# Differential attention: one wide product per head instead of two, and norm factors that travel through DRAM

## The chip, the cores and the metric

The kernel runs on one core of a Trainium2 chip. The metric is the device time of one execution in microseconds. The profile of one execution is used beside it; its times count from the first instruction.

The engines are TensorE (PE, with its weight loads PEld), VectorE (DVE), ScalarE (ACT), GpSimd (POOL) and SyncE (SP). SP issues all DMAs of the kernel before. Matrix products go into PSUM banks of 128 partitions by 512 floats; the other engines read them from there.

## The reference

The model is one layer of an encoder, run on two sequences of 512 tokens (`x_prompt`, `x_sample`), width 1024. Three branches work on the normalised input: a state space scan, a differential attention, and a cross attention to 256 memory tokens. Each goes through its up-projection and a gate; their sum goes through an output projection and a feed-forward part. The change lies in the differential attention:

```python
def block(qblk):                       # 128 queries at a time
    s = jnp.einsum('bqhd,bkhd->bhqk', qblk, k).astype(jnp.float32) * scale
    probs = jax.nn.softmax(s, axis=-1).reshape(Bn, DIFF_HEADS, 2, Q_BLOCK, L)
    w = probs[:, :, 0] - lam * probs[:, :, 1]
    return jnp.einsum('bhqk,bkhe->bqhe', w.astype(v.dtype), v)
...
o = _rmsnorm(o, subln_g) * (1.0 - lambda_init)     # over the 128 columns of a head
```

There are 4 heads, each with two score maps of depth 64 and values of depth 128. After the weighted sum over v each token's 128 values of a head are divided by their root mean square: one factor for each token, head and sequence.

## The kernel before, in words

Matrices are split into a high and a low part in the reduced float type (fp32r), and each product is three matmuls (high by high, high by low, low by high). `split` makes the parts: a copy on ScalarE for the high part, a subtraction on DVE for the low one. `weight` (L143 to L150) loads a weight tile through SP into one of two buffers wf and splits it into wh and wl.

The differential attention is one loop over `steps`: 4 heads, 2 sequences and 4 query tiles of 128 make 32 steps. A (head, sequence) pair takes four steps in a row. Within a pair, `qt` runs from 0 to 3. The work of a step is spread over several turns of the loop:

- `scores` runs on every second turn, for two query tiles at a time. PE makes the scores of both maps, DVE the row maxima (nb), ScalarE the exponentials, DVE the weighted difference of the maps (e0).
- `turn` transposes the 128x512 difference on PE, four transposes into one bank of the tag tr, and splits it into pH and pL.
- `outputs` multiplies v by those. It works on two query tiles at once: 12 matmuls of 256 columns, run at every odd `qt`. The two halves share one PSUM bank (oo), and after the second half ScalarE copies it to `osb`, a 128x512 tile with the head's depth on the partitions and the tokens along the columns.
- `squares`, two turns after a pair's last step, transposes `osb`, so that ScalarE can sum the squares of a token's values; the result `ss` is 128x4, with a token on each partition.
- `normed`, three turns after a pair's last step, calls `factor`: square root on ScalarE, reciprocal on DVE (rs, 128x4), and then four transposes on PE, which lay the factor of every token along the columns and repeat it on all 128 partitions, in a second bank of the tag tr (bc). DVE multiplies `osb` by it, and SP stores the result to bD in DRAM.

Between these parts `fill(n)` puts other matmuls into PE's list from a queue: projections of q and k of the next heads, projections of v, gate projections, and towards the end of the loop the merge of the other branches. `fill(n)` takes about n matmuls of 512 columns. While this loop is built, PE keeps its instructions in the order in which they are written (`PE.on`). The order on the other engines and on SP is chosen by a scheduler, which may be held back with `issue_after`; `queued()` places a DMA after the last weight load.

There are two PSUM banks of the tag tr (shared by `scores`, `turn`, `squares` and the broadcast of the factors), two of mm for the filling matmuls, three of sc and one of oo. `osb` has two buffers, and so has the tag acc, which `squares` uses for its squares.

After the loop, `merge_in(1)` loads bD[1] back from DRAM.

Of the kernel before, what the change touches and what calls it, by code (L numbers as in the profile page):

```python
# [10 lines left out]
F32 = mybir.dt.float32  # L11
F32R = mybir.dt.float32r
I32 = mybir.dt.int32
AF = mybir.ActivationFunctionType
ALU = mybir.AluOpType
# [4 lines left out]
P = 128  # L20
L = 512
# [51 lines left out]
def encoder(ctx: ExitStack, tc: tile.TileContext, a, out):  # L73
    nc = tc.nc
    V, S, PO, PE = nc.vector, nc.scalar, nc.gpsimd, InOrder(tc, nc.tensor)
# [8 lines left out]
    rp = ctx.enter_context(tc.tile_pool(name="rp", bufs=2))  # L84
# [3 lines left out]
    def open_tags(es, side=None, **tags):  # L88

        for tag, n in tags.items():  # L90
            pools[tag] = es.enter_context(tc.tile_pool(name=tag, bufs=n, side=side, reuse_waits="tile"))
# [10 lines left out]
    xp_es, phase = ExitStack(), ExitStack()  # L102
    open_tags(xp_es, side="right", xp=2 * KD)
    drp = ctx.enter_context(tc.tile_pool(name="drp", bufs=1, space=DRAM))

    def slot(tag, shape=(P, NT), dt=F32, name="sl"):
        return pools[tag].tile(list(shape), dt, tag=tag, name=name)

    def bank(tag="mm"):
        return pools[tag].tile([P, 512], F32, tag=tag, name="bk" + tag)  # L110

    def aux():
        return bank("tr")
# [17 lines left out]
    def split(hi, lo, src, scale=None):  # L131

        if scale is None:
            h = S.copy(hi, src)  # L134
            l_ = V.tensor_tensor(out=lo, in0=src, in1=hi.bitcast(F32), op=ALU.subtract)  # L135
        else:
            h = S.activation(out=hi, in_=src, func=AF.Copy, scale=scale)
            l_ = V.scalar_tensor_tensor(out=lo, in0=src, scalar=scale, in1=hi.bitcast(F32), op0=ALU.mult, op1=ALU.subtract)
        return h, l_
# [23 lines left out]
    def proj(src, hi, lo, nk=KD, seqs=(0, 1)):  # L163


        wh, wl = weight(src, nk * P)
        outs = []
        for s in seqs:
            cs = slice(s * L, (s + 1) * L)
            outs.append(bank())  # L170
            for k in range(nk):
                mm3(outs[-1:], wh, wl, [(hi[k][:, cs], lo[k][:, cs])], k, nk)
        return outs
# [10 lines left out]
    def new_acc():  # L184
        return rp.tile([P, L], F32, tag="acc", name="acc", bufs=2)

    def rstd(acc, n, nt=4):


        ss = aux()  # L190
        for t in range(nt):
            PE.matmul(ss[:, t : t + 1], acc[:, t * P : (t + 1) * P], onec[:, 0:1], start=(t == 0), stop=(t == nt - 1))
        return factor(ss, n, nt)

    def factor(ss, n, nt=4, bias=epsc):

        rs = rp.tile([P, 4], F32, tag="rs", name="rs", bufs=4)
        S.activation(out=rs[:, :nt], in_=ss[:, :nt], func=AF.Sqrt, scale=1.0 / n, bias=bias)
        V.reciprocal(rs[:, :nt], rs[:, :nt])
        bc = aux()  # L200
        for t in range(nt):
            PE.transpose(bc[:, t * P : (t + 1) * P], rs[:, t : t + 1].broadcast_to([P, P]), ident)
        return rs, bc
# [26 lines left out]
    def sums(src, tag="wb", ss=None, ts=range(4)):  # L230

        nonlocal last_sq
        if ss is None:
            ss = rp.tile([P, 4], F32, tag="ss", name="ss", bufs=3)
        for t in ts:
            tk = slot(tag, [P, DM], name="tk")
            nc.sync.dma_start(tk, src[t])
            last_sq = S.activation(out=tk, in_=tk, func=AF.Square, accum_out=ss[:, t : t + 1])
        return ss
# [53 lines left out]
    def queued():  # L293

        return tc.issue_after(last_w.ins)
# [54 lines left out]
    with yielding(last_s):  # L350
        x_norm(0, norm[0], range(5, 8))
        _, bc = factor(ss1, DM)
# [30 lines left out]
    for t2 in range(2):  # L383
# [3 lines left out]
        for s in range(NS):  # L387
            for t in range(2):
                o = bank()
# [126 lines left out]
    with behind():  # L516
# [3 lines left out]
        rs_, bc = factor(sums(a["memN"], "ld"), DM)  # L520
# [4 lines left out]
    for t in range(4):  # L525
        o = proj(a["w_glu"][t], zh, zl, 4)
# [32 lines left out]
    g04 = cst.tile([P, 1], F32, name="g04")  # L559
# [38 lines left out]
    def fill(n):  # L598
        nonlocal owed
        owed += n  # L600
        while owed > 0 and queue:
            r = next(queue[0], None)
            if r is None:
                queue.pop(0)
            else:
                owed -= r
        if not queue:
            owed = 0

    def finish(g):  # L610
        while any(g is g_ for g_ in queue):
            fill(1)
# [75 lines left out]
    steps = [(h, s, lt) for h in range(4) for s in range(NS) for lt in range(4)]  # L688
    es, pT = {}, {}
    AHEAD = 2  # L690
    for i in range(-AHEAD, len(steps) + 1):
        if i + AHEAD < len(steps):
            h, s, lt = steps[i + AHEAD]
# [9 lines left out]
            last_e = last_x, V.tensor_scalar_mul(e, e, r)  # L703
            es[i + AHEAD] = e
        fill(9 if i == 0 else 5)
        if 0 <= i < len(steps):
            h, s, lt = steps[i]
# [3 lines left out]
            tr = aux()  # L711
# [4 lines left out]
        if i > 0 and steps[i - 1][2] == 3:  # L716
            h, s, _ = steps[i - 1]
            pTh, pTl = pT.pop((h, s))
            oo = bank("oo")
# [5 lines left out]
            osb = xa.tile([P, L], F32, tag="osb", name="xosb", bufs=1)  # L725
# [7 lines left out]
    phase.close()  # L733


    open_tags(phase, v2=2, qk=12, pT=4)
    aes = ExitStack()
    ap_ = aes.enter_context(tc.tile_pool(name="att", bufs=2, reuse_waits="tile"))
    acol = aes.enter_context(tc.tile_pool(name="acol", bufs=2, reuse_waits="tile"))
# [21 lines left out]
    qk = {}  # L761
# [40 lines left out]
    def first_in():  # L802
        b0.append(merge_in(0, ["qk", "qk", "qk", "v"]))
        yield 0
# [25 lines left out]
    s0, ss, osb = {}, {}, {}  # L830
# [22 lines left out]

    def turn(i):
        h, s, qt = steps[i]
        if qt % 2 == 0:
            pT[h, s, qt // 2] = tuple(slot("pT", [P, 4, 2 * P], F32R, n_) for n_ in ("pH", "pL"))
        e0 = es.pop(i)
        tr = aux()
        for j in range(4):  # L860
            PE.transpose(tr[:, j * P : (j + 1) * P], e0[:, j * P : (j + 1) * P], ident)
        ps = slice(qt % 2 * P, qt % 2 * P + P)
        split(*(p_[:, :, ps] for p_ in pT[h, s, qt // 2]), tr.rearrange("p (j q) -> p j q", j=4))

    def outputs(i):

        h, s, qt = steps[i]
        if h == 2 and s == qt - 1 == 0:
            finish(v1_)
        vh, vl = (v1 if h >= 2 else v0)[s]  # L870
        vs = slice((h % 2) * P, (h % 2) * P + P)
        pH, pL = pT.pop((h, s, qt // 2))
        if qt == 1:
            osb[h, s] = bank("oo")
        od = osb[h, s][:, qt // 2 * 2 * P : (qt // 2 + 1) * 2 * P]
        for j in range(4):
            PE.matmul(od, vh[:, j, vs], pH[:, j, :], start=(j == 0), stop=False)
            PE.matmul(od, vh[:, j, vs], pL[:, j, :], start=False, stop=False)
            PE.matmul(od, vl[:, j, vs], pH[:, j, :], start=False, stop=(j == 3))
        if qt == 3:  # L880
            o_ = rp.tile([P, L], F32, tag="nsq", name="osb", bufs=2)
            S.copy(o_, osb[h, s])
            osb[h, s] = o_

    def squares(i):
        h, s, _ = steps[i]
        tr = aux()
        ss[h, s] = rp.tile([P, 4], F32, tag="ss", name="ss", bufs=3)
        for t in range(4):
            PE.transpose(tr[:, t * P : (t + 1) * P], osb[h, s][:, t * P : (t + 1) * P], ident)  # L890
        sq = new_acc()
        for t in range(4):
            S.activation(out=sq[:, t * P : (t + 1) * P], in_=tr[:, t * P : (t + 1) * P], func=AF.Square,
                         accum_out=ss[h, s][:, t : t + 1])
        V.scalar_tensor_tensor(out=s0[h, s], in0=s0[h, s], scalar=EPS * P, in1=s0[h, s], op0=ALU.mult, op1=ALU.mult)
        V.tensor_tensor(out=ss[h, s], in0=ss[h, s], in1=s0[h, s], op=ALU.add)

    def normed(i):
        h, s, _ = steps[i]
        _, bc = factor(ss[h, s], P, bias=0.0)  # L900
        V.scalar_tensor_tensor(out=osb[h, s], in0=osb[h, s], scalar=g04, in1=bc, op0=ALU.mult, op1=ALU.mult)
        nc.sync.dma_start(bD[1, h, :, s * L : (s + 1) * L], osb[h, s])

    n = len(steps)
    for i in range(-1, n + 3):
        if i % 2 and i + 1 < n:
            scores(i + 1)
        if i == 22:
            queue.insert(1, first_in())
        fill(10 if i < n - 1 else 16)  # L910
        if 0 <= i < n:
            turn(i)
        if 0 < i <= n and steps[i - 1][2] % 2:
            outputs(i - 1)
        fill(10)
        if 1 < i <= n + 1 and steps[i - 2][2] == 3:
            squares(i - 2)
        if i > 2 and steps[i - 3][2] == 3:
            normed(i - 3)
    aes.close()  # L920
    while queue:
        fill(24)
# [212 lines left out]
    for i in range(KFF):  # L1135
# [14 lines left out]
        ps = products(i, w)  # L1150
        p0 = next(ps)
        if i == 0:
            for s in range(NS):
                _, bc = rstd(accs[s], DM)
# [92 lines left out]
    for v, (m, lo_, hi_) in enumerate(VISITS):  # L1247
        ps = [bank() for _ in range(6)] + [aux()]
# [22 lines left out]
        ps = iter(ps)  # L1271
# [62 lines left out]
    for c, n in ((0, L), (L, L // 2), (L + L // 2, L // 2)):  # L1334
        acc = new_acc()
        for m in range(KD):
# [6 lines left out]
            o = bank()[:, :n]  # L1343
# [12 lines left out]
            if m == KD - 3:  # L1356
                ss = aux()
# [435 lines left out]
```

## Time and profile before

| | us |
|---|---|
| median of 3 runs | 1598.61 |
| lowest, highest | 1598.05, 1599.04 |
| the profiled execution's own time | 1599.28 |
| its span, from first to last instruction | 1597.5 |
| the loop of the differential attention, roughly | from 494 to 770 |

Granted clock of TensorE in the profiled execution: 0.998 of full speed.

How to read the rows in the next part: rows of groups give an engine, an operation, the tile written and the tile read, the shapes, the count, the busy time and the mean duration of one in nanoseconds. Rows in order of time give the start, the length, and in brackets the engine's idle time before it with what ended it. A matmul's own length overlaps with the next one's, so what PE pays for one is the distance from its start to the next start. Rows of DMAs give the issuing queue, the size of one, and the median time from issue to landing. "x12" behind a row counts the instructions merged in it.

### The profile page before, as it was taken

Reading aid. Unit: us, or ns where it says so; the run is one execution under the profiler, and the core shown is the slowest. Engines: PE = TensorE matmul, PEld = TensorE weight load, DVE = VectorE, ACT = ScalarE, POOL = GpSimd, SP = SyncE. Lnnn points to the kernel's source line nnn. Section 1 sums busy time; section 2 is a strip of 40 time slices with the busy share of each in tenths; the row PEclk is TensorE's granted clock in tenths of the full one; section 3 lists DMA queues with packets and bytes.
Section 4 is the critical chain, followed back from the end, with each engine's and each line's share of the span. In section 5 each row is a group of like instructions: output and inputs, shape, how many; then the busy total and the mean of one; then the engine's idle time right before and its main releaser. Section 6 shows DMA issues by size and latency. Waiting matters only on the chain.

```text
span 1597.5 us, 21606 instructions
## 1 busy us (share of the span) xinstructions
PE 1579.1 (99%) x7838; PEld 1314.8 (82%) x7838; DVE 1163.7 (73%) x1856; ACT 636.8 (40%) x1140; POOL 542.6 (34%) x449
## 2 busy tenths in 40 slices
PE   9999999999999999999999999999999999999997
PEld 7888788888898789878878878888888888788877
DVE  7976997067774776775365578888898778998654
ACT  6544313265552465573123443323333224233323
POOL 0010100001333220300443366666665553444553
PEclk9999999999999999999999999999999999999999
DMA  9544523676762111253454432333332223985222
GB/s 366 174 159 152 175 94 123 182 261 213 262 224 102 46 55 40 73 178 133 138 190 140 144 108 89 123 122 129 119 116 109 81 91 115 355 332 196 75 67 106
DMA packets 104890, 237.84 MB, mean 149 GB/s; under 512 B 13520, under 2 KB 45008, under 8 KB 104784
## 3 DMA queue, kind: packets, MB, share of 16 engines
q1 hardware_dynamic: 104784, 236.47, 43.4%
q8 instruction: 61, 1.00, 0.2%
q14 instruction: 45, 0.37, 0.1%
HBM read 165.16 MB, written 71.27 MB: 148 GB/s over the span
## 4 chain that ended last, share of the span: by engine, by line
PE 89%; DVE 5%; issue 2%; DMA 2%; POOL 1%; ACT 1%; SPq 0%; POOLq 0%; DVEq 0%; ACTq 0%
PE bkmm L66 78%; PE bktr L66 3%; DVE tl L135 2%; PE bkoo L66 2%; PE bktr L69 2%; PE bksc L66 1%; PE bktr L1627 1%; PE bktr L1598 1%; PE bktr L1688 0%; PE bktr L1686 0%; PE bktr L1687 0%; PE bktr L1566 0%; DMA acc<-in_w_fo 0%; DMA mt<-in_memT 0%; DMA fl<-aD 0%
## 5 line engine op out<-in xcount | busy, mean ns | idle before, releaser
L66 PE MATMUL bkmm<-xh,wh 128*128 128x512 f32 x640 | 254.7, 398 | 0.0
L66 PE MATMUL bkmm<-xh,wl 128*128 128x512 f32 x640 | 251.1, 393 | 0.0
L66 PE MATMUL bkmm<-xl,wh 128*128 128x512 f32 x640 | 250.5, 391 | 0.0
L66 PE MATMUL bkmm<-tl,wh 128*128 128x512 f32 (+1 forms) x621 | 241.3, 389 | 1.4 <-DVE tl L135 1.4
L66 PE MATMUL bkmm<-th,wl 128*128 128x512 f32 (+1 forms) x621 | 241.1, 389 | 1.0 <-DVE wl L135 1.0
L66 PE MATMUL bkmm<-th,wh 128*128 128x512 f32 (+1 forms) x621 | 241.3, 389 | 0.0
L134 ACT CAST wh<-wf 128x1024 fp32r<-128x1024 f32 (+1 forms) x134 | 117.9, 880 | 220.8 <-PE bkmm L66 183.2
L135 DVE TENSOR_TENSOR wl<-wf,wh 128x1024 fp32r<-128x1024 f32 (+1 forms) x134 | 146.5, 1093 | 48.8 <-ACT wh L134 33.5
L66 PE MATMUL bkmm<-th,w 128*128 128x512 f32 x432 | 141.4, 392 | 3.5 <-DVE up L1102 2.0
L66 PEld LDWEIGHTS bkmm<-xh,wl 128*128 128x128 f32 x640 | 120.2, 188 | 26.6 <-issue 1.3
L66 PEld LDWEIGHTS bkmm<-xh,wh 128*128 128x128 f32 x640 | 120.4, 188 | 26.4 <-issue 3.4
L66 PEld LDWEIGHTS bkmm<-xl,wh 128*128 128x128 f32 x640 | 120.5, 188 | 22.6 <-issue 0.4
L66 PEld LDWEIGHTS bkmm<-tl,wh 128*128 128x128 f32 x621 | 116.6, 188 | 26.2 <-DVE tl L135 2.1
L66 PEld LDWEIGHTS bkmm<-th,wl 128*128 128x128 f32 x621 | 116.6, 188 | 25.6 <-DVE wl L135 1.9
L66 PEld LDWEIGHTS bkmm<-th,wh 128*128 128x128 f32 x621 | 116.6, 188 | 23.7
L1166 POOL TENSOR_TENSOR up<-up,acc 128x512 f32<-128x512 f32 x44 | 84.2, 1931 | 87.4 <-DVE up L1102 87.4
L454 POOL TENSOR_TENSOR raw<-raw 128x128 f32<-128x128 f32 x28 | 15.2, 546 | 285.0 <-DVE nb L545 206.5
L66 PEld LDWEIGHTS bkmm<-th,w 128*128 128x128 f32 x432 | 80.9, 188 | 24.9 <-DVE up L1102 4.5
L793 POOL TENSOR_TENSOR mg<-mg,gl 128x1024 f32<-128x1024 f32 x16 | 43.5, 2720 | 138.1 <-DVE gl L789 138.1
L66 PE MATMUL bkmm<-tl,w 128*128 128x512 f32 x216 | 84.2, 390 | 0.0
L66 PE MATMUL bkmm<-yh,wh 128*128 128x512 f32 x192 | 75.9, 397 | 0.8 <-DVE gl L789 0.8
L1165 ACT ACTIVATE ac<-gf 128x512 f32<-128x512 f32 x44 | 27.8, 633 | 122.5 <-DVE gf L1164 63.5
(651 smaller groups left out, 3580.8 us busy)
## 6 DMA issues: line engine op xcount, KB each, us to landing
wf<-in_w_in SPq DMA_DIRECT2D x40, 512.0 KB, 4.1
wD<-hl SPq DMA_DIRECT2D x28, 512.0 KB, 2.9
w<-wD SPq DMA_DIRECT2D x28, 512.0 KB, 4.8
gD<-gt SPq DMA_DIRECT2D x24, 512.0 KB, 2.8
gl<-gD SPq DMA_DIRECT2D x24, 512.0 KB, 3.4
wf<-in_w_fg SPq DMA_DIRECT2D x22, 512.0 KB, 3.7
wf<-in_w_fu SPq DMA_DIRECT2D x22, 512.0 KB, 3.6
aD<-ac SPq DMA_DIRECT2D x22, 512.0 KB, 3.0
```

What stands on the lines that cost most here:

```text
L66: return self.put(self.eng.matmul(*args, **kw))
L69: return self.put(self.eng.transpose(*args, **kw))
L134: h = S.copy(hi, src)
L135: l_ = V.tensor_tensor(out=lo, in0=src, in1=hi.bitcast(F32), op=ALU.subtract)
L454: PO.tensor_tensor(out=a22, in0=a21, in1=a22, op=ALU.add)
L793: PO.tensor_tensor(out=mg[m], in0=mg[m], in1=gt, op=ALU.add)
L1165: last_t = S.activation(out=ac[:, cs], in_=gf, func=AF.Tanh, scale=0.5)
L1166: PO.tensor_tensor(out=up, in0=up, in1=accs[s], op=ALU.mult)
L1598: PE.matmul(kp[64 * hf : 64 * hf + 48, g * 144 : (g + 1) * 144], l_[:, 2 * hf + g, :], o_[:, 4 * g4 + 2 * hf + g, :], start=(l_ is lr48), ...
L1627: PE.matmul(ps[:, g * P : (g + 1) * P], w_[:, gg * P : (gg + 1) * P], u_[:, 8 * o + gg, :], start=True, stop=True)
```

## The change

The products with v of a pair are made in one run of 12 matmuls of 512 columns, after all four query tiles have been transposed. The transposed probabilities of a pair lie in one tile of 512 columns for each part; there are two such tiles (high and low) instead of four of half the width. The products come before the transposes of the next pair's first tile, and the fill around them is shifted by four matmuls (14 and 6 instead of 10 and 10).

The norm factors of all pairs but the last take another way. `factors` makes rs as before, three turns after the pair's last step, without the transposes on PE. One turn later SP writes it to DRAM (`spread_out`), transposed, so that 512 factors lie in a row: 512 single floats from 128 partitions. One turn after that the row is read back on all 128 partitions into a tile of the tag acc (`spread_in`); this DMA is issued by ScalarE, behind the exponentials of the last scores. Two turns after that `normed` multiplies `osb` by it. The last pair keeps `factor` and its transposes.

```diff
-    open_tags(phase, v2=2, qk=12, pT=4)
+    open_tags(phase, v2=2, qk=12, pT=2)
...
     def turn(i):
         h, s, qt = steps[i]
-        if qt % 2 == 0:
-            pT[h, s, qt // 2] = tuple(slot("pT", [P, 4, 2 * P], F32R, n_) for n_ in ("pH", "pL"))
+        if qt == 0:
+            pT[h, s] = tuple(slot("pT", [P, 4, L], F32R, n_) for n_ in ("pH", "pL"))
...
-        ps = slice(qt % 2 * P, qt % 2 * P + P)
-        split(*(p_[:, :, ps] for p_ in pT[h, s, qt // 2]), tr.rearrange("p (j q) -> p j q", j=4))
+        ps = slice(qt * P, qt * P + P)
+        split(*(p_[:, :, ps] for p_ in pT[h, s]), tr.rearrange("p (j q) -> p j q", j=4))
...
     def outputs(i):
...
-        pH, pL = pT.pop((h, s, qt // 2))
-        if qt == 1:
-            osb[h, s] = bank("oo")
-        od = osb[h, s][:, qt // 2 * 2 * P : (qt // 2 + 1) * 2 * P]
+        pH, pL = pT.pop((h, s))
+        od = bank("oo")
         for j in range(4):
             PE.matmul(od, vh[:, j, vs], pH[:, j, :], start=(j == 0), stop=False)
             PE.matmul(od, vh[:, j, vs], pL[:, j, :], start=False, stop=False)
             PE.matmul(od, vl[:, j, vs], pH[:, j, :], start=False, stop=(j == 3))
-        if qt == 3:
-            o_ = rp.tile([P, L], F32, tag="nsq", name="osb", bufs=2)
-            S.copy(o_, osb[h, s])
-            osb[h, s] = o_
+        osb[h, s] = rp.tile([P, L], F32, tag="nsq", name="osb", bufs=2)
+        S.copy(osb[h, s], od)
...
+    rD = drp.tile([2 * 4, 4, P], F32, name="rD")
+    far = {}
+
+    def factors(i):
+        h, s, _ = steps[i]
+        if i == n - 1:
+            far[h, s] = factor(ss[h, s], P, bias=0.0)[1]
+            return
+        rs = far[h, s] = rp.tile([P, 4], F32, tag="rs", name="rs", bufs=4)
+        S.activation(out=rs, in_=ss[h, s], func=AF.Sqrt, scale=1.0 / P, bias=0.0)
+        V.reciprocal(rs, rs)
+
+    def spread_out(i):
+        h, s, _ = steps[i]
+        with queued():
+            nc.sync.dma_start(rD[2 * h + s].rearrange("t p -> p t"), far[h, s])
+
+    def spread_in(i):
+        h, s, _ = steps[i]
+        far[h, s] = new_acc()
+        with tc.issue_after(last_e[0].ins):
+            nc.scalar.dma_start(far[h, s], rD[2 * h + s : 2 * h + s + 1].rearrange("o t p -> o (t p)").broadcast_to([P, L]))
+
     def normed(i):
         h, s, _ = steps[i]
-        _, bc = factor(ss[h, s], P, bias=0.0)
-        V.scalar_tensor_tensor(out=osb[h, s], in0=osb[h, s], scalar=g04, in1=bc, op0=ALU.mult, op1=ALU.mult)
+        V.scalar_tensor_tensor(out=osb[h, s], in0=osb[h, s], scalar=g04, in1=far[h, s], op0=ALU.mult, op1=ALU.mult)
         nc.sync.dma_start(bD[1, h, :, s * L : (s + 1) * L], osb[h, s])
...
-        fill(10 if i < n - 1 else 16)
+        due = 0 < i <= n and steps[i - 1][2] == 3
+        fill((10 if i < n - 1 else 16) + 4 * due)
+        if due:
+            outputs(i - 1)
         if 0 <= i < n:
             turn(i)
-        if 0 < i <= n and steps[i - 1][2] % 2:
-            outputs(i - 1)
-        fill(10)
+        fill(10 - 4 * due)
         if 1 < i <= n + 1 and steps[i - 2][2] == 3:
             squares(i - 2)
+        if i > 6 and steps[i - 7][2] == 3:
+            with tc.issue_after(last_e[1].ins):
+                normed(i - 7)
         if i > 2 and steps[i - 3][2] == 3:
-            normed(i - 3)
+            factors(i - 3)
+            if i == n + 2:
+                normed(i - 3)
+        if i > 3 and i - 4 < n - 1 and steps[i - 4][2] == 3:
+            spread_out(i - 4)
+        if i > 4 and i - 5 < n - 1 and steps[i - 5][2] == 3:
+            spread_in(i - 5)
```

More of the change, by code (lines that the diff above doesn't have):

```diff
@@ L861, in turn @@
             PE.transpose(tr[:, j * P : (j + 1) * P], e0[:, j * P : (j + 1) * P], ident)
-        ps = slice(qt % 2 * P, qt % 2 * P + P)
-        split(*(p_[:, :, ps] for p_ in pT[h, s, qt // 2]), tr.rearrange("p (j q) -> p j q", j=4))
+        ps = slice(qt * P, qt * P + P)
+        split(*(p_[:, :, ps] for p_ in pT[h, s]), tr.rearrange("p (j q) -> p j q", j=4))
     def outputs(i):
-        h, s, qt = steps[i]
-        if h == 2 and s == qt - 1 == 0:
+        h, s, _ = steps[i]
+        if h == 2 and s == 0:
             finish(v1_)
@@ L896, in squares @@
         V.tensor_tensor(out=ss[h, s], in0=ss[h, s], in1=s0[h, s], op=ALU.add)
+    rD = drp.tile([2 * 4, 4, P], F32, name="rD")
[13 more added lines that the diff above has]
+    def spread_in(i):
+        h, s, _ = steps[i]
+        far[h, s] = new_acc()
+        with tc.issue_after(last_e[0].ins):
+            nc.scalar.dma_start(far[h, s], rD[2 * h + s : 2 * h + s + 1].rearrange("o t p -> o (t p)").broadcast_to([P, L]))
     def normed(i):
         h, s, _ = steps[i]
-        _, bc = factor(ss[h, s], P, bias=0.0)
-        V.scalar_tensor_tensor(out=osb[h, s], in0=osb[h, s], scalar=g04, in1=bc, op0=ALU.mult, op1=ALU.mult)
+        V.scalar_tensor_tensor(out=osb[h, s], in0=osb[h, s], scalar=g04, in1=far[h, s], op0=ALU.mult, op1=ALU.mult)
         nc.sync.dma_start(bD[1, h, :, s * L : (s + 1) * L], osb[h, s])
```

## The prediction

> **What bounds the kernel now.** I read the page first, then the stretches of time around the differential attention, then who PE waits for there, then the chain that ended last, then single rows on PE, ScalarE (ACT), VectorE (DVE) and SyncE's queue (SP). The page:
>
> ```profile
> span 1597.5 us, 21606 instructions
> PE 1579.1 (99%) x7838; PEld 1314.8 (82%) x7838; DVE 1163.7 (73%) x1856; ACT 636.8 (40%) x1140; POOL 542.6 (34%) x449
> PEclk9999999999999999999999999999999999999999
> PE 89%; DVE 5%; issue 2%; DMA 2%; POOL 1%; ACT 1%; SPq 0%; POOLq 0%; DVEq 0%; ACTq 0%
> ```
>
> PE is busy for 99% of the span at a full clock, and the chain that ended last is 89% PE. All edits lie in the loop that runs from about 494 to 770 us. Busy time in that stretch, by engine, in the order PE, PEld, DVE, ACT, POOL, then clock, DMA share, GB/s; and below it the only wait of PE's matmuls in this part that the profile names:
>
> ```profile
> 494.00:770.00 276.00, 275.20 (x1552) 228.12 (x1551) 182.97 (x339) 136.54 (x313) 51.04 (x33) 1.00 0.25 85
> ...
> PE bktr L69 <- DVE osb L901: 0.8, 1, 0.8
> ```
>
> PE has work for 275.2 of 276 us, ScalarE for half of them and the DMA engines for a quarter. In this loop PE takes its instructions in the order written. So what leaves PE's list leaves the time, one for one, as long as nothing makes PE wait; and what is added to ScalarE, SP and the DMAs costs nothing as long as it is not late.
>
> **The products with v.** Before, each of eight (head, sequence) pairs has two runs of 12 products of 256 columns; after, one run of 12 with 512. The chain that ended last gives runs with their length and count, start to start:
>
> ```profile
> 542.93 1.43 PE bkoo L66 x12
> 556.64 1.44 PE bkoo L66 x12
> 745.61 5.49 PE bkmm L66 x24
> 767.10 32.69 PE bkmm L66 x144
> ```
>
> The first two are runs of 256 columns: 1.44/12 = 0.120 us each. The last two are 512 columns: 32.69/144 = 0.227, 5.49/24 = 0.229. Sixteen runs are 16 x 1.44 = 23.0 us; 96 products of 512 columns are 96 x 0.228 = 21.9. Saved: 1.1 us (1.0 with the slower row, 1.2 with the faster).
>
> By the Trainium skill (TensorE: Matmul & The Clock Gate, Back-to-back issue gap) a warm matmul takes N/2.4 ns plus 2.5 ns, so two of 256 would lose only 2.5 ns on one of 512, 0.24 us in all, and the whole sum would be 4.1 instead of 5.0. The trace disagrees on the pitch of both shapes (120 and 227 to 229 ns against 109 and 216), so I go by the rows.
>
> The first matmul behind a group of transposes is slower, but that loss moves with the transposes: in the new order the fill behind them pays it instead of the products. Cost zero.
>
> **The broadcast of the norm factors.** Four transposes per pair copy the factors (rs) over the partitions. Seven pairs lose them. PE's starts without such a group ahead of the scores, and with one:
>
> ```profile
> 546.72 0.39 PE L66 MATMUL bkmm<-xh,wl 128*128 128x512 f32 x1
> 547.03 0.49 PE L66 MATMUL bktr<-rh 64*128 64x512 f32 x1
> ...
> 573.28 0.39 PE L66 MATMUL bkmm<-xh,wl 128*128 128x512 f32 x1
> 573.50 0.60 PE L69 MATMUL bktr<-ident,rs 128*128 128x128 f32 x4
> 574.03 0.50 PE L66 MATMUL bktr<-rh 64*128 64x512 f32 x1
> ```
>
> From the last fill matmul to the scores it is 0.31 us without and 0.75 with: 0.44 a group, 7 x 0.44 = 3.1 us saved.
>
> **The one named stall.** The broadcast also occupies one of the two PSUM banks of the tag tr until DVE has multiplied. Once that was late:
>
> ```profile
> 715.67 0.40 PE L66 MATMUL bkmm<-yh,wl 128*128 128x512 f32 x1
> 716.83 0.66 PE L69 MATMUL bktr<-ident,e 128*128 128x128 f32 x4 [0.77 <-DVE osb L901]
> ...
> 722.80 0.39 PE L66 MATMUL bkmm<-yh,wl 128*128 128x512 f32 x1
> 723.03 0.60 PE L69 MATMUL bktr<-ident,e 128*128 128x128 f32 x4
> ```
>
> The transposes start 1.16 us after the fill where 0.23 is usual: 0.93 lost. After, no bank is held for the broadcast, and the bank those transposes take belongs to an earlier step. What is late next is DVE itself in these merge steps, so I count 0.8; bounds are the whole 0.93 and a new wait of the same size (-0.9).
>
> **The new trip through DRAM.** Per pair: SP writes the 128x4 factors, ScalarE issues the read that spreads them into a 128x512 tile, DVE multiplies two steps after that, and SP's store follows. Queue by queue:
>
> SP gains seven issues. Each needs factors that DVE has already made. Built, the new write stands where the store of the same pair stood or behind a weight load, and each store stands about where the store of the following pair stood. One issue of SP is 0.33 us:
>
> ```profile
> 735.52 0.33 SPq L146 DMA_DIRECT2D wf<-in_w_up  x1
> 743.81 0.33 SPq L146 DMA_DIRECT2D wf<-in_w_up  x1
> 749.74 0.33 SPq L146 DMA_DIRECT2D wf<-in_w_up  x1
> wf<-in_w_up SPq DMA_DIRECT2D x24, 256.0 KB, 3.3
> ```
>
> Weight loads leave 6 to 8 us apart, each when a split frees one of two buffers, so the load of 735.52 is first needed about when the split that issues 749.74 starts, some 13 us later, and it lands in 3.3. An SP held for a few us delays no matmul. Cost zero; without that cover it would be 7 x 0.33 = 2.3 us.
>
> ScalarE gains seven issues (2.3 us at SP's duration; the trace has none of ScalarE's own, and at half or double that it still fits) on an engine idle for half the stretch. The dearer part is the wait: ScalarE stands at the read until the write has landed, and queued behind it are the cast of the transposed weights (pH) and the next weight's cast (wh), on which DVE's remainders and then PE hang. How long a write has: the factors of the first pair are ready at 571.83, and the read stands behind the softmax of the next scores, whose last entry ends at 578.54.
>
> ```profile
> 571.65 0.18 DVE L199 RECIPROCAL rs<-rs 128x4 f32<-128x4 f32 x1 [0.82 <-ACT rs L198]
> 578.33 0.21 ACT L548 ACTIVATION_READ_ACCUMULATOR e<-bksc,nb 128x1 f32 x1
> ...
> 737.33 0.18 DVE L199 RECIPROCAL rs<-rs 128x4 f32<-128x4 f32 x1 [1.35 <-ACT rs L198]
> 742.26 0.62 ACT L134 CAST wh<-wf 128x512 fp32r<-128x512 f32 x1 [4.48 <-PE bkmm L66]
> ```
>
> That is 6.7 us. The tightest is the seventh: its read stands right behind one pH cast, without new scores; ready at 737.51, and the next ScalarE work, a weight cast, had anyway to wait for PE until 742.26: 4.7 us free.
>
> How long the write takes no row shows: 512 runs of 4 bytes. Nearest rows:
>
> ```profile
> bD<-osb SPq DMA_DIRECT2D x8, 256.0 KB, 2.0
> gD<-gk SPq DMA_DIRECT2D x16, 2.0 KB, 1.4
> yD<-y__2902 SPq DMA_DIRECT2D x8, 64.0 KB, 2.0
> w__2733<-gD SPq DMA_DIRECT2D x8, 64.0 KB, 3.8
> ```
>
> Lower end 1.4 us (2 KB, as here, in 32 runs of 64 bytes). Upper end, if time goes with the number of runs: the last row has 128 runs of 512 bytes, so 1.4 + 4 x (3.8 - 1.4) = 11.0. I take 2.0, because the payload is 2 KB and even 256 KB of this tile lands in that. At 2.0 ScalarE does not wait: cost zero, and the read (256 KB, some 2 to 4 us) has nearly two steps.
>
> By the Trainium skill (DMA: Bandwidth & Descriptors, Rules for kernel authors) a non-contiguous last dimension becomes one descriptor per element; this write is such a one. That speaks for the upper end, and no row here tells what 512 descriptors cost.
>
> **The multiply on DVE** reads the factors from SBUF instead of PSUM; the weighting line has that form:
>
> ```profile
> L851 DVE SCALAR_TENSOR_TENSOR e<-e,r x32: 731/752/1381, 526.5 to 732.2; 128x512 f32<-128x512 f32 x32
> L901 DVE SCALAR_TENSOR_TENSOR osb<-osb,g,bktr x8: 734/744/748, 574.1 to 767.3; 128x512 f32<-128x512 f32 x8
> ```
>
> 0.75 us against 0.74, at worst 1.38. It is now bound ahead of nothing that PE waits for. Buffers: the tile of a pair is stored two steps before the next user of its slot. The probability tiles are two of double size, one set only; ScalarE's first write of the next pair comes behind transposes that PE takes after the products, so no extra wait. The last pair keeps its transposes: no change.
>
> **Sum.** 1.1 + 3.1 + 0.8 = 5.0 us. The profiled execution took 1599.28 us (span 1597.5); it becomes 1594.3. The median of the runs shown, 1598.61, is 0.67 below the profiled time, so the forecast is 1593.6. From no change, 0.2% or 3.2 us (1595.4 to 1601.8) is about what a measurement of this kernel tells.
>
> **Rivals.** *The gain is eaten by new waits (within 0.2%).* Where merge units fill the gaps, DVE and ScalarE work through loads (yl behind yh), and the longer gap between products changes when banks come free. Two or three waits like that of 716.83, 0.9 each, would leave 5.0 - 0.8 - 2.2 = 2.0: 1596.6. For it: that wait came from DVE's order, and the built order there differs. Against: PE waited once in 276 us. Chance 0.16.
>
> *The write lands late and holds ScalarE (slower).* At 11.0 us the first six reads come 4.3 us late each, the seventh 6.4. Slack behind them is about 2 us, from the remainder to the products:
>
> ```profile
> 580.81 0.68 DVE L135 TENSOR_TENSOR pL<-bktr,pH 128x512 fp32r<-128x512 f32 x1
> 583.67 1.44 PE bkoo L66 x12
> ```
>
> 6 x 2.3 + 4.4 = 18.2 us lost: 1611.8. It decides from a landing of about 6.7 + 2 + 5.0/7 = 9.4 us. For it: four times the runs of the slowest small row. Against: 2 KB only, and the 64-byte runs landed in 1.4. Chance 0.10. The rule of the Trainium skill on the last dimension (same page and section) would work through this mechanism.
>
> *The wide product saves nothing* (512 columns would take twice the 256): 3.9 instead of 5.0, 1594.7; 144 matmuls in a row at 0.227 speak against it. It lies inside the forecast's own range.
>
> **How the numbers follow.** The forecast has 0.74: 1592.5 (the whole stall, the faster pitch, the run-to-run spread) to 1595.4. The rival within 0.2% has 0.16, the slower one 0.10. For 8 in 10 the range needs a part of the second: 1592.3 to 1597.2. Faster 0.74, same 0.16, slower 0.10.
>
> **What would show it.** Right: 96 products of 512 columns at a pitch near 0.228; 32 fewer transposes would be wrong, 28 is the number; no PE wait on osb; ScalarE reads that follow their write by over 2 us and idle nowhere before a pH cast. Wrong: PE waiting for pH, pL or wl in this loop, or the write landing over 6.7 us after its issue.

## The result and the profile after

| | median, us | lowest to highest | runs |
|---|---|---|---|
| before | 1598.68 | 1598.05 to 1599.40 | 6 |
| after | 1608.96 | 1607.29 to 1612.16 | 6 |

The ratio after to before is 1.0066, 95% interval [1.0053, 1.0079]: the change costs 10.6 us (0.0066 x 1599), between 8.5 and 12.6. The forecast was a gain of 5.0. The page of the profiled execution of the changed kernel (its own time is 1612.16 us, 3.2 above the median):

```profile
span 1610.3 us, 21390 instructions
...
PE 1581.1 (98%) x7714; PEld 1310.2 (81%) x7714; DVE 1162.0 (72%) x1856; ACT 636.2 (40%) x1140; POOL 546.7 (34%) x449
...
PEclk9999999999999999998999999999999999999999
...
PE 85%; DMA 5%; DVE 5%; issue 2%; ACT 2%; POOL 1%; SPq 0%; ACTq 0%; POOLq 0%; DVEq 0%
```

PE has 124 instructions fewer (7838 before), and still the span is 12.8 us longer. In the chain that ended last the DMAs went from 2% to 5%, and one slice of the clock shows an 8. That slice lies at the end of the loop. Two rows of busy time by engine in a stretch (PE, PEld, DVE, ACT, POOL, then clock, DMA share, GB/s) give the size. First the kernel before, from the start of the loop to 830 us:

```profile
494.00:830.00 336.00, 334.36 (x1811) 276.63 (x1810) 214.26 (x378) 150.54 (x331) 78.33 (x43) 1.00 0.31 102
```

The same stretch after, 12 us longer because the stage ends that much later:

```profile
494.00:842.00 348.00, 334.31 (x1686) 269.85 (x1685) 212.69 (x378) 147.86 (x329) 78.37 (x43) 0.99 0.34 104
```

PE stands idle for 1.6 us before and 13.7 after: 12.1 more. Who waited for what between 494 and 830 us in the changed kernel (total, times, longest), PE's matmuls first and the waits for the new tiles below:

```profile
PE bkmm L66 <- DVE mg L789: 9.5, 2, 7.4
PE bkmm L66 <- DVE wl L135: 1.8, 1, 1.8
PE bkoo L66 <- ACT pH L134: 1.0, 1, 1.0
...
ACT wh L134 <- DMA rD<-rs: 9.6, 1, 9.6
ACT pH L134 <- DMA rD<-rs: 7.0, 2, 3.9
ACT vh L134 <- DMA rD<-rs: 1.3, 1, 1.3
DVE osb L919 <- DMA acc<-rD: 10.5, 1, 10.5
```

The wait for osb, the only one that the prediction quoted, is gone, and others stand in its place. ScalarE stands for the write of the factors (rD<-rs) four times by name. A fifth time the profile names another releaser, but the read leaves at 667.54, right behind the landing at 667.46, and ScalarE has then been idle for 4.5 us up to its next cast. The reason is in the rows of DMA issues (size of one, median time from issue to landing):

```profile
rD<-rs SPq DMA_DIRECT2D x7, 2.0 KB, 10.1
acc<-rD ACTq DMA_DIRECT2D x7, 256.0 KB, 4.8
```

The write of 2 KB takes 10.1 us to land (8.3 to 10.9 over the seven), twice the time of the read of 256 KB behind it. None of the seven reads leaves before its write has landed; each leaves within 0.1 us of the landing.

The dearest case is the seventh pair, in order of time, on SP, ScalarE, DVE and PE (start, length, instruction, in brackets the idle time before it and what ended it):

```profile
742.79 0.18 DVE L904 RECIPROCAL rs<-rs 128x4 f32<-128x4 f32 x1 [1.35 <-ACT rs L903]
743.00 0.37 SPq L909 DMA_DIRECT2D rD<-rs  x1
...
752.44 0.33 ACTq L915 DMA_DIRECT2D acc<-rD  x1
752.86 0.62 ACT L134 CAST wh<-wf 128x512 fp32r<-128x512 f32 x1 [9.62 <-DMA rD<-rs]
...
757.26 0.75 DVE L919 SCALAR_TENSOR_TENSOR osb<-osb,g,acc 128x512 f32<-128x512 f32 x1 [10.52 <-DMA acc<-rD]
757.93 0.68 DVE L135 TENSOR_TENSOR wl<-wf,wh 128x512 fp32r<-128x512 f32 x1
758.53 0.68 DVE L789 SCALAR_TENSOR_TENSOR mg<-gl,bkmm 128x512 f32<-128x512 f32 x1
...
751.56 0.39 PE L66 MATMUL bkmm<-yh,wl 128*128 128x512 f32 x1
759.36 0.76 PE L66 MATMUL bkmm<-yh,wh 128*128 128x512 f32 x1 [7.41 <-DVE mg L789]
759.92 0.63 PE L66 MATMUL bkmm<-yl,wh 128*128 128x512 f32 x1
760.35 0.63 PE L66 MATMUL bkmm<-yh,wl 128*128 128x512 f32 x1
...
764.62 0.58 PE L66 MATMUL bkmm<-yh,wh 128*128 128x512 f32 x1
765.03 0.40 PE L66 MATMUL bkmm<-yl,wh 128*128 128x512 f32 x1
```

The busy times of the stretch behind the wait (PE, PEld, DVE, ACT, POOL, then clock, DMA share, GB/s):

```profile
754.80:765.00 10.20, 5.64 (x13) 4.46 (x14) 3.89 (x7) 0.00 (x0) 0.00 (x0) 0.50 0.52 182
```

Read it from the top. The factors are ready at 742.97 and SP writes at once. ScalarE reaches its read and stands there until 752.44, with the weight cast wh behind it. The read lands at 757.24. DVE stands for it, since the multiply of osb comes ahead of the remainder wl and the merge product mg in DVE's order; mg frees a bank at 759.2, and PE goes on at 759.36, 7.6 us late. Then a second loss follows: up to 764.62 PE starts a matmul every 0.43 us instead of every 0.23, which is 11 x 0.20 = 2.2 us, and 0.5 more at the two ends of that stretch. The granted clock is 0.50 from 754.80 to 765.00. By the Trainium skill (TensorE: Matmul & The Clock Gate, What's actually happening) the array's clock falls to a half after an idle window of about 3.4 us and comes back after as long a busy one. The 7.4 us of idle time and the starts 0.43 us apart behind it agree; the slow stretch of 5.7 us is longer than that.

The sum for this trace: 12.1 us of idle time and 2.7 of half clock, less the 4.2 that the shorter list of PE should save (1.1 and 3.1, from the prediction), is 10.6. The two profiled spans differ by 12.8, so 2.2 us of this execution are not accounted for: either PE's shorter list saved less than 4.2 here, or something else was lost. The medians differ by 10.3, and that this is close to the sum proves nothing, since the profiled execution lies 3.2 above its median.

### The profile page after: what moved, and what is told of

Same layout as the page of the kernel before. It is cut to its first block, busy times and chain, and to the rows that moved or that the text cites. A ratio compares the mean times of both kernels' runs of the same rounds, so it can differ in the third digit from the quotient of the medians.

```text
span 1610.3 us, 21390 instructions
## 1 busy us (share of the span) xinstructions
PE 1581.1 (98%) x7714; PEld 1310.2 (81%) x7714; DVE 1162.0 (72%) x1856; ACT 636.2 (40%) x1140; POOL 546.7 (34%) x449
## 4 chain that ended last, share of the span: by engine, by line
PE 85%; DMA 5%; DVE 5%; issue 2%; ACT 2%; POOL 1%; SPq 0%; ACTq 0%; POOLq 0%; DVEq 0%
PE bkmm L66 74%; PE bktr L66 3%; DMA rD<-rs 2%; PE bkoo L66 2%; DVE tl L135 1%; PE bktr L69 1%; PE bksc L66 1%; PE bktr L1655 1%; PE bktr L1626 1%; DMA mt<-in_memT 0%; PE bktr L1715 0%; PE bktr L1716 0%; PE bktr L1714 0%; PE bktr L1594 0%; DVE nb L543 0%
## 5 line engine op out<-in xcount | busy, mean ns | idle before, releaser
L66 PE MATMUL bkmm<-yl,wh 128*128 128x512 f32 x192 | 75.8, 395 | 0.0
```

Of the source, the lines that this page charges most:

```text
L66: return self.put(self.eng.matmul(*args, **kw))
```

## The experiments

There are three theories. **A**: the write of 512 runs lands about 10 us after its issue, and who waits for it (ScalarE, at the read) holds up the rest. **B**, the rival: the new order of the products makes DVE and ScalarE late. **C**, a second rival, about the place of the loss: the small runs make the other transfers late, whoever waits. Ratios are to the kernel before on the same chip; a per cent is 16 us.

### The two parts one by one

The products of 512 columns alone, with the factors spread by PE's transposes as before (`e1_products`):

```diff
-            factors(i - 3)
...
-            spread_out(i - 4)
...
-            spread_in(i - 5)
+            normed(i - 3)
...
+        _, bc = factor(ss[h, s], P, bias=0.0)
```

> The products of 512 columns alone; the factors are spread by transposes on PE as before. If the late write of the factors is the whole cause (theory A), this keeps only the first term of the sum: 1.1 us faster, 1597.5, or up to 2 us if the one stall on the multiply also moves. If the new order of products and transposes makes DVE and ScalarE late (theory B), it is slower than before by most of the 10 us, with PE waits on pH, pL or mg.

The other part alone: two runs of 256 columns as before, the factors through DRAM (`e2_factors`):

```diff
-        due = 0 < i <= n and steps[i - 1][2] == 3
-        fill((10 if i < n - 1 else 16) + 4 * due)
-        if due:
-            outputs(i - 1)
+        fill(10 if i < n - 1 else 16)
         if 0 <= i < n:
             turn(i)
+        if 0 < i <= n and steps[i - 1][2] % 2:
+            outputs(i - 1)
```

> The way through DRAM alone; the products stay in two runs of 256 columns. Theory A: about as slow as the whole change and 1 us more, 1608 to 1611, with one PE wait of 5 to 8 us near the seventh read. Theory B: faster than before by 3 to 4 us, 1595.

Measured: the products alone 1598.47 us against 1600.07, ratio 0.9988 [0.9980, 0.9997], a gain of 1.9 us (0.5 to 3.2). The trip alone 1611.89, ratio 1.0073 [1.0061, 1.0086], a loss of 11.7 us. PE's longest wait in the loop with the products alone:

```profile
PE bktr L66 <- DVE pL L135: 1.5, 1, 1.5
```

So the products gave what the forecast said (1.1), within their interval, and B falls: the whole loss comes with the trip through DRAM. The trip alone loses about as much more than the whole change (11.7 against 10.6) as the products were to save.

### The same bytes in longer runs

The whole change, but the tile in DRAM keeps the four factors of a partition side by side: 128 runs of 16 bytes instead of 512 of 4. The multiply then reads its factors with a stride of four (`e4_runs16`):

```diff
-    rD = drp.tile([2 * 4, 4, P], F32, name="rD")
+    rD = drp.tile([2 * 4, P, 4], F32, name="rD")
-            nc.sync.dma_start(rD[2 * h + s].rearrange("t p -> p t"), far[h, s])
+            nc.sync.dma_start(rD[2 * h + s], far[h, s])
```

> The change, but DRAM holds the factors partition by partition: the write has 128 runs of 16 bytes instead of 512 of 4, the read stays one row, and DVE's multiply reads the factors with a step of four. Theory A (the landing goes with the number of runs): the write lands in 2 to 4 us, ScalarE does not stand, and the time is that of the forecast, 1593.5 to 1595. If the landing goes with the kind of write (small pieces into DRAM, whatever their number), it stays near 10 us and the time at 1607 to 1610.

Measured: 1599.13 us, ratio 0.9994 [0.9985, 1.0003]. The loss is gone, but the 1593.5 to 1595 that theory A expected are missed. The row of the write, and PE's largest wait in the loop:

```profile
rD<-rs SPq DMA_DIRECT2D x7, 2.0 KB, 1.8
...
PE bkmm L66 <- DVE mg L789: 2.3, 1, 2.3
```

The payload is the same 2 KB; a quarter of the runs lands in 1.8 us instead of 10.1 (1.4 to 6.2 over the seven). The multiply with its stride takes 1.13 us instead of 0.75. The packets of the whole execution, in the changed kernel:

```profile
DMA packets 109594, 239.69 MB, mean 149 GB/s; under 512 B 17328, under 2 KB 48816, under 8 KB 109488
```

and with runs of 16 bytes:

```profile
DMA packets 106906, 239.69 MB, mean 150 GB/s; under 512 B 14640, under 2 KB 46128, under 8 KB 106800
```

The difference is 2688 = 7 x (512 - 128): one packet for each run. That agrees with the rule that the prediction quoted from the Trainium skill (DMA: Bandwidth & Descriptors, Rules for kernel authors). Fewer runs are longer runs here, 16 bytes instead of 4, and no run keeps one of the two fixed: whether the landing goes with the number of runs or with their shortness is not shown. What is left against the forecast is 4 us (a gain of 1.0 instead of 5.0, and the interval includes zero); below, part of it is traced to waits in the merge steps.

### Fewer pairs

Six of the eight pairs through DRAM would keep the trip away from the merge steps, where it cost most. Here the last two pairs keep their transposes (`e3_six`), and in a second kernel the six use runs of 16 bytes (`e8_six16`):

```diff
-        if i == n - 1:
+        if i >= n - 5:
             far[h, s] = factor(ss[h, s], P, bias=0.0)[1]
```

> The whole change, but the last two pairs keep the transposes on PE, so six writes are left and the tightest read is gone. The trace of the change shows PE idle 7.6 us behind the seventh read and 2.6 us lost to the slower matmuls after that. If the seventh alone makes the loss: 10 us less than the whole change, about the time of before. If every write costs alike (17 us of PE waits over seven): 2.5 us less than the whole change, still 8 us slower than before.

> Runs of 16 bytes and the last two pairs on PE: both cures together. Theory A and C agree: no wait behind the factors is left. 1.1 us for the products and 6 x 0.44 = 2.6 for the transposes would give 3.7 us less than before; the waits on mg and yl in the merge steps (about 2 us in the run with 16-byte runs) may take half of that.

Measured: 1602.79 us, ratio 1.0014 [1.0005, 1.0023], and 1598.38, ratio 0.9992 [0.9983, 1.0001]. Without the seventh pair the loss shrinks from 10.6 us to 2.2: most of it lay there, as the rows above show. With longer runs it vanishes again; of the 3.7 us that the shorter list of PE was to give there, 1.3 are measured, and the interval includes zero.

### The write alone

The kernel before, with the seven writes of 512 runs added and nobody reading them (`e5_write_only`), and the same with 128 runs of 16 bytes (`e9_write16`):

```diff
+        with queued():
+            nc.sync.dma_start(rD[2 * h + s].rearrange("t p -> p t"), rss[i])
```

> The kernel before, with only the seven writes of the factors added; nobody reads them, the transposes on PE stay. Theory A: the write still takes about 10 us to land, nobody waits, and the time is that of before, 1598.7, within 1 us. Theory C (512 small pieces block the queue, and the weight loads behind them come late): the weight loads behind the writes land several us later, and the time rises by 5 us or more.

> The kernel before with seven writes that nobody reads, as 128 runs of 16 bytes. The same seven writes as 512 runs of 4 bytes cost 6.6 us. If it is the number of runs that delays the transfers behind them (theory C), this costs under 1 us. If any additional write between the loads shifts them into the stall near 715 us, it costs 4 us or more again.

Measured: 1606.63 us, ratio 1.0046 [1.0033, 1.0060], and 1599.51, ratio 0.9996 [0.9987, 1.0004]. A write that nothing waits for costs 7.4 us, and with a quarter of the runs nothing that the interval tells from zero. Theory A alone does not explain that. Rows of SP and of ScalarE around the sixth write (512 runs), and PE's wait:

```profile
707.94 0.39 SPq L904 DMA_DIRECT2D rD<-rs  x1
708.45 0.42 SPq L776 DMA_DIRECT2D yt<-bD  x1
...
718.63 1.06 ACT L137 ACTIVATE yh<-yt 128x1024 fp32r<-128x1024 f32 x1 [5.19 <-DMA yt<-bD]
...
PE bktr L69 <- DVE osb L910: 5.7, 1, 5.7
```

The load of yt, issued right behind the write, is there 10.2 us later; in the kernel before, loads of yt land in 4.3 us in the median. ScalarE stands for it, then DVE (the remainder yl, and osb behind it), then PE for 5.7 us. That is C: what stands behind the write is late.

### The read one turn later

If only the waiting counted (A), more room would cure it. The read and the multiply are moved one turn on (`e7_later`):

```diff
-        if i > 4 and i - 5 < n - 1 and steps[i - 5][2] == 3:
-            spread_in(i - 5)
+        if i > 5 and i - 6 < n - 1 and steps[i - 6][2] == 3:
+            spread_in(i - 6)
```

> The whole change, with the read and the multiply of a pair one turn later (read two turns after the write, not one). The writes and their runs stay. Where the cost is ScalarE standing at the read (theory A), the waits of pH and of the weight casts on the write go for the first six pairs, and the time falls by 3 to 5 us or more, if the seventh gains its turn too by up to 10. Where the cost is what the write does to the queue (theory C), the time stays within 2 us of the whole change.

Measured: 1608.84 us, ratio 1.0051 [1.0038, 1.0064]. ScalarE no longer waits for the write anywhere in the loop, and the time stays: a loss of 8.2 us (6.1 to 10.2), which overlaps with that of the whole change (8.5 to 12.6). PE's wait, and the link of the chain of work that ended last that caused it (start, us, what):

```profile
PE bkmm L66 <- DVE mg L789: 11.8, 1, 11.8
...
710.15 13.72 DMA yt<-bD
```

A load of yt issued 0.4 us behind the sixth write takes 13.7 us. The wait that was cured came back at another place, by C.

### Whose queue

Is it SP's queue that is held up, or the DMA engines themselves? The unread write of 512 runs, now issued by ScalarE (`e11_write_act`):

```diff
-            nc.sync.dma_start(rD[2 * h + s].rearrange("t p -> p t"), rss[i])
+            nc.scalar.dma_start(rD[2 * h + s].rearrange("t p -> p t"), rss[i])
```

> The kernel before plus the seven unread writes of 512 runs, but issued by ScalarE instead of SP (the twin of the run with the unread writes on SP, 1606.6). If the small runs hold up what is behind them on the same queue only, SP's loads of yt land in 3 to 6 us again, PE has no wait of 5.7 us and the time is 1597 to 1600. If they hold up the DMA engines that all queues share, loads issued in the 10 us after a write land late as before and the time is 1604 to 1608. The landing of the write itself stays 9 to 11 us by both.

and the same edit on top of the later read (`e10_later_act`; the write that its expectation calls the seventh is the sixth):

> The whole change with the read and the multiply one turn later (that run took 1608.8, with PE waiting 11.8 us for a merge product because a load of yt stood 13.7 us behind the seventh write on SP's queue), and now the write issued by ScalarE instead of SP. If the hold is of the queue: that load lands in 3 to 7 us, PE's wait falls to 2.5 us or less, time 1595 to 1600. If it is of the DMA engines: the wait stays at 8 to 12 us, time 1604 to 1610.

Measured: 1604.27 us, ratio 1.0019 [1.0011, 1.0028], and 1609.62, ratio 1.0057 [1.0042, 1.0071]. The write on ScalarE's queue and the chain's link for SP's load, in the first:

```profile
708.52 0.37 ACTq L904 DMA_DIRECT2D rD<-rs  x1
...
708.15 8.80 DMA yt<-bD
```

and in the second:

```profile
709.70 0.38 ACTq L909 DMA_DIRECT2D rD<-rs  x1
...
711.42 10.66 DMA yt<-bD
```

Loads on SP's queue are late although the write is on another queue, even the one issued 0.4 us ahead of it. Another queue saves part of the unread write's cost (3.0 us instead of 7.4) and nothing of the later read's. In the second, PE's wait for the merge product is 7.0 us, between the two forecasts (2.5 or less, 8 to 12); a wait of 2.4 for another tile and two stretches of half clock stand beside it. So the hold is at least in part in what the queues share. By the Trainium skill (DMA: Bandwidth & Descriptors, Issuing engines are not separate DMA queues) transfers of all issuing engines run on the same 16 DMA engines and interleave there. These two runs agree; which shared part holds the loads they do not show.

### Who waits

The read issued by SP, so that SP stands for the write and ScalarE never does (`e6_read_sp`):

```diff
-            nc.scalar.dma_start(far[h, s], rD[...].broadcast_to([P, L]))
+            nc.sync.dma_start(far[h, s], rD[...].broadcast_to([P, L]))
```

> The whole change, but SP issues the read of the factors, so SP stands until the write has landed and ScalarE never does. If the loss comes from ScalarE standing alone (theory A), and the cover I gave SP holds, no ScalarE cast waits for the write, the 7.4 us of PE before the merge product go, and the time is 1596 to 1600 us. If what stands behind the write is late whoever waits (theory C), then the loads behind it on SP stand even longer than in the changed kernel: weight loads and the loads of yt are late, PE still loses 8 to 14 us in the loop, and the time is 1604 to 1612.

Measured: 1608.65 us, ratio 1.0049 [1.0036, 1.0062]. Waits of SP and DVE in the loop, and two links of the chain:

```profile
SPq L915 <- DMA rD<-rs: 58.4, 7, 10.4
DVE osb L919 <- DMA acc<-rD: 12.2, 1, 12.2
...
738.77 8.52 DMA rD<-rs
747.36 5.14 DMA acc<-rD
```

SP stands for 58 us and ScalarE for none, and the seventh pair still keeps DVE at the multiply for 12.2 us, with the merge product behind it. The time is the one forecast by C, but here the wait is A's. Theory A holds for the length of the landing, not for ScalarE: whoever carries the wait, the chain from write to read to multiply is 14 us long.

### What is left of the forecast

The later read and multiply with runs of 16 bytes (`e12_later16`), that is `e7_later` with the edit of `e4_runs16`:

> The same later read and multiply, the write on SP, but in 128 runs of 16 bytes. No wait for the write by either theory. If what is left above the forecast is the order of DVE in the merge steps (rival 1), 1595 to 1599, with one PE wait of about 2 us for a merge product; if the strided multiply is what is late, nothing changes against the run with 16-byte runs and the read in its place (1599.1 against 1599.9 for the kernel before).

Measured: 1597.93 us against 1600.56, ratio 0.9988 [0.9978, 0.9997], a gain of 1.9 us (0.5 to 3.5). PE's largest wait in the loop, and DVE's rows ahead of its end:

```profile
PE bkmm L66 <- DVE mg L789: 3.1, 1, 3.1
...
714.41 0.68 DVE L543 TENSOR_REDUCE nb<-bktr 128x1 f32<-128x512 f32 x1
...
715.61 1.22 DVE L138 SCALAR_TENSOR_TENSOR yl<-yt,yh 128x1024 fp32r<-128x1024 f32 x1
716.74 1.28 DVE L543 TENSOR_REDUCE nb<-bksc 128x1 f32<-128x512 f32 x2
...
718.60 0.68 DVE L789 SCALAR_TENSOR_TENSOR mg<-gl,bkmm 128x512 f32<-128x512 f32 x1
```

DVE is busy without a break; the row maxima (nb) and a remainder (yl) come ahead of the merge product for which PE stands. No multiply of osb is among them. Behind the wait PE starts eight matmuls 0.43 us apart, another 1.6 us; this execution lies 3.0 us above the run's median. This is the mechanism of the rival of the prediction that the gain is eaten by waits in the merge steps (1596.6, a gain of 2.0). With a cheap write that rival would have been close: this run gained 1.9, the one with the read in its old place 1.0. This kernel and the products alone are the only two that are faster than before, by about 0.12% each; none reaches the forecast. As the products alone give as much, no run shows a net gain from taking the transposes off PE.

## Why the prediction was wrong

The step that failed is one term, the time of the write: "I take 2.0, because the payload is 2 KB and even 256 KB of this tile lands in that." It measured 10.1 us in the median (8.3 to 10.9), five times as much. The working had both ends: 1.4 from 32 runs of 64 bytes, and 11.0 "if time goes with the number of runs". The upper end was right within a tenth. I chose the lower by payload, although bytes did not order the rows that I quoted: the row of 64 KB in 128 runs took 3.8 us, a row of 256 KB 2.0. The rule of the Trainium skill beside them spoke for the upper end too. Between ends so far apart a chance of 0.10 for the slower case was too small.

The points one by one:

- **Products with v, 1.1 us saved: right.** Their own run gained 1.9 (0.5 to 3.2), and in its trace they start 0.227 to 0.229 us apart.
- **Transposes, 3.1 us saved: right by count.** PE has 124 instructions fewer: 96 of the products and 28 transposes. No run shows this gain, since each carries the trip too; with a cheap write and the later read both parts together gain 1.9, no more than the products alone.
- **The stall on osb, 0.8 us: gone as foreseen, and replaced** by waits for mg, wl and pH of 12.3 us in all.
- **"The write lands late and holds ScalarE": this was the outcome.** The rival gave 1611.8; the median is 1608.96. Its decision point, a landing over 9.4 us, was passed by the median. Its distribution was off: it had six stands of ScalarE of 4.3 us and one of 6.4 (by its own terms, 11.0 less 4.7, 6.3); the trace has four of 1.3 to 4.5, one of 9.6 and two reads before which ScalarE was at work until the landing. What it lacked is the half clock behind the long stand.
- **The multiply "is now bound ahead of nothing that PE waits for": wrong.** In the seventh pair it stands ahead of the merge product, and passes its wait for the read on to PE. The read took 4.8 us in the median (3.7 to 6.7), not 2 to 4, and in the seventh pair the multiply has no two steps of room: with runs of 16 bytes DVE still stands 2.2 us for it there, only without harm to PE.
- **SP's seven writes at cost zero: wrong.** I counted issues of 0.33 us and a cover of some 13 us for weight loads, and asked what is late if SP is held. SP's issues were not what was held; the transfers around the write were. In the run with the unread write those are loads of yt, and it alone costs 7.4 us. In the changed kernel the loads of yt leave ahead of the sixth write and land in 5.2 to 6.4 us, and it is the three loads of gl behind it that are late (8.3 to 9.7 us, 3.4 in the median before).
- **New waits in the merge steps: right as a rival.** With runs of 16 bytes the measured gains are 1.0 to 1.9 us instead of 5.0.

In the changed kernel itself the chain of the seventh pair (A) holds most: 7.4 of the 12.1 us of idle time, and the half clock. The cost of the late loads (C) is shown in other kernels, and cannot be added to it: the write alone costs 7.4, and moving the read takes one wait away and brings the other.

## What to carry to other kernels

Price a small DMA by its separate runs, how many and how short, not by its bytes, and if the trace has no row with as many runs, forecast from the dear end. A slow write is paid twice, by whoever waits for it and by the transfers issued around it, on other queues too; so look at the loads that PE's next products hang on, and not only at the reader. Before a tile takes a way through DRAM, choose the layout there so that each partition writes one run.

## What was not expected of the hardware

**The landing is long after the packets.** DMA packets in the changed kernel from the end of the seventh write's issue on, for 0.9 us:

```profile
DMA packets 617, 0.16 MB, mean 186 GB/s; under 512 B 538, under 2 KB 538, under 8 KB 617
```

and in the 5.4 us after that, with a load of gl that SP issued at 746.77 and its time to landing:

```profile
DMA packets 8, 0.02 MB, mean 3 GB/s; under 512 B 7, under 2 KB 7, under 8 KB 7
...
gl<-gD SPq DMA_DIRECT2D x1, 512.0 KB, 9.9
```

The tiny packets are recorded within 1.25 us of the issue. Then the DMA engines show nearly nothing for 5.4 us, though a load of 512 KB waits for most of the second half of it, and the write is reported landed at 752.4. What happens in that time the records do not show; that 512 runs of 4 bytes take this long where 128 of 16 do not, and that loads issued around them are late on both queues, is measured.

**Half clock after shorter waits too.** In the kernel with six pairs and runs of 16 bytes the clock halved behind a wait of 2.1 us (granted clock 0.50 from 722.30 to 725.70); PE's rows:

```profile
719.28 0.39 PE L66 MATMUL bkmm<-yh,wl 128*128 128x512 f32 x1
721.80 0.51 PE L66 MATMUL bkmm<-yh,wh 128*128 128x512 f32 x1 [2.13 <-DVE mg L789]
...
722.84 0.63 PE L66 MATMUL bkmm<-yh,wh 128*128 128x512 f32 x1
723.27 0.63 PE L66 MATMUL bkmm<-yl,wh 128*128 128x512 f32 x1
```

Starts 0.43 us apart follow, as after the wait of 7.4 us. With six pairs and runs of 4 bytes waits of 1.3 and 0.2 us (at 695.95 and 696.67) were followed by six of them from 698.11 on. But after the wait of 2.3 us with seven pairs and runs of 16 bytes PE went on at 0.23, and after the one of 2.1 at 725.61 in the changed kernel at 0.24. So the 3.4 us of the Trainium skill (same page and section as above) are no safe bound here, and the length of the wait alone does not decide; what does stays open.
